# Where the operands of the large products begin in SBUF: a two-layer trunk with other offsets

## The chip, the core and the metric

The kernel runs on one core of a Trainium2 chip. Its metric is the device time of one execution in microseconds. Three runs of the kernel before gave 1264.4, 1265.62 and 1267.93 us, median 1265.62. One more execution, taken with the hardware profiler, is the one that every row below comes from.

The engines are named as the profile names them: PE is TensorE's matrix products, PEld is TensorE's loading of the stationary operand (it runs beside PE), DVE is VectorE, ACT is ScalarE, POOL is GpSimd, and SP is the engine that starts nearly all DMAs. SBUF is the on-chip memory of 128 partitions from which TensorE reads both operands; a tile's address below is its byte offset within each partition.

## The reference

Two residual layers on one sequence of 512 tokens with 1024 channels, in float32. Cut to what matters here, `h @ w` are the large products:

```python
mod = c_act @ ada_w[layer] + ada_b[layer]          # six shifts, scales and gates
h = rms_norm(x, norm_mix[layer]) * (1.0 + scale1) + shift1
if layer % 2 == 0:                                 # gated convolution and HGRN2 recurrence
    y = mixer_conv_hgrn(h, w_in_ab[j], conv_w[j], hg_norm[j], lower_bounds[layer], w_out_ab[j])
else:                                              # stick-breaking attention, 16 heads of 64
    y = mixer_stick_breaking(h, w_qkv[j], q_norm[j], k_norm[j], w_out_c[j])
x = x + gate1 * y
h = rms_norm(x, norm_mlp[layer]) * (1.0 + scale2) + shift2
x = x + gate2 * (jnp.square(jax.nn.relu(h @ mlp_w1[layer])) @ mlp_w2[layer])
```

## The kernel before

**Products.** Activations lie transposed, channels on the partitions and the 512 tokens along the row. Every large product is made of three: the weights and the activations are each split into a high part, rounded to TensorE's fast float32 form (`F32R`), and a low part, the rest. `mm3` (L281) issues, for one 128x128 block of weights, high weights by high activations (L284), high weights by low activations (L285) and low weights by high activations (L286). In each the weights are the stationary operand, loaded into the array, and the activations the moving operand, streamed through it. A product over all tokens is 512 columns wide; where a stage is cut into two halves of the tokens, so that the second half of the work before it can still be under way, it is 256 wide. In the attention's value products (`v_stream`, L1427 to L1429) and those of the first mixer (`v_g`, L737 to L739) the sides are exchanged: activations are stationary and weights move.

**Stages.** First norm and input products (`start`, L505); mixer of layer 0, whose chunked recurrence puts small products between the large ones (L701 to L947); its output projection, half of it in token halves (`proj`, L954); first MLP (`mlp_head` in halves, then `mlp` over 512 tokens, its last three outputs in halves); attention (L1088 to L1506); second MLP. From `start` on, the order of PE's instructions is the program's own or that of a list scheduler (`Graph`, L107), which orders by estimated durations and knows no addresses.

**Weights.** Each of the weight tiles, 128x1024 float32 (512 KB), is loaded by SP into one of three `raw` buffers, rounded by ACT into `whi` (L274) and subtracted by DVE into `wlo` (L275), each in a ring of four buffers.

**Where tiles lie.** A pool lays out its tiles one behind the other in the order of their first allocation, and the next pool begins where the last one ends: `base` (residual `x`, activations `hh`/`hl`, norms, constants), `wp` (`raw`, `whi`, `wlo`), `adap` (modulation), then `mix`, `mlp0`, `att` and `mlp1`, which take turns. So the size of every tile ahead sets where a tile begins. Four tiles matter only for that or are moved by the change: `gap0` (L319, 8 floats) and `gap1` (L320, 24 floats), which nothing reads or writes; `sel` (L248, 2048 bytes per partition), the stationary operand of eight products of layer 0's mixer (L899, L900); and `lvl` (L249, 448 bytes), masks that DVE reads in the same mixer (L805, L818).

Below, a tile's **place** is its address modulo 256 bytes. A block of 128 weight columns is 512 bytes, and a half of the tokens is 1024, so the blocks and halves of a tile have the place of the tile.

Of the kernel before, what the change touches and what calls it, by code (L numbers as in the profile page):

```python
# [12 lines left out]
F32 = mybir.dt.float32  # L13
F32R = mybir.dt.float32r
# [3 lines left out]
U8 = mybir.dt.uint8  # L18
# [4 lines left out]
P = 128  # L23
# [67 lines left out]
class Ring:  # L91
# [5 lines left out]
    def new(self):  # L97
        return Handle(self)
# [127 lines left out]
def trunk(tc, x_d, c_d, rep_d, small_d, const_d, ada_d, ws_d, win_d, wv_d, woab_d, w1_d, w2_d, wqk_d, wvc_d, woc_d, out_d):  # L226
# [6 lines left out]
    def pool(name, space=None, stack=es):  # L233
        kw = {} if space is None else {"space": space}
        return stack.enter_context(tc.tile_pool(name=name, bufs=1, reuse_waits="tile", **kw))

    base = pool("base")
    wp = pool("wp")
# [6 lines left out]
    modc = base.tile([P, 96], F32, name="modc")  # L245
    gsc = base.tile([P, 32], F32, name="gsc")
    lb = base.tile([P, 12], F32, name="lb")
    sel = base.tile([P, 512], F32R, name="sel")  # L248
    lvl = base.tile([P, 7 * 64], U8, name="lvl")  # L249
    ident = cons[:, C_ID:C_ID + P]  # L250
    ones = base.tile([P, P], F32, name="ones")
    o32 = cons[:, C_O32:C_O32 + 32]
# [16 lines left out]

    def split_w(raw, of=None):  # L270

        new = lambda n, tag: of[0].tile([P, 1024], F32R, name=n, tag=tag) if of else wp.tile([P, 1024], F32R, name=n, tag=n, bufs=4)
        hi, lo = [new(n, of and of[1 + i]) for i, n in enumerate(("whi", "wlo"))]
        act.copy(hi, raw)  # L274
        dve.tensor_tensor(lo, raw, hi.bitcast(F32), op=ALU.subtract)  # L275
        return hi, lo

    def load_w(src, of=None):
        return split_w(raw_w(src), of)
# [36 lines left out]
    eps_b = base.tile([P, 1], F32, name="eps_b")  # L316
    ls_b = base.tile([P, 1], F32, name="ls_b")

    base.tile([P, 8], F32, name="gap0")  # L319
    wp.tile([P, 24], F32, name="gap1")  # L320

    def rsqrt_act(ms, a, y):

# [16 lines left out]
    mp = pool("mix", stack=mx_s)  # L340
    mps_s = ExitStack()
    mps = pool("mps", PSUM, mps_s)

    def acc():
        return mps.tile([P, T], F32, name="acc", tag="acc", bufs=4)
# [55 lines left out]
    def late_constants():  # L401
        ctmp = wp.tile([P, 1024], F32, name="ctmp", tag="raw", bufs=3)
        act.dma_start(ctmp[:, :C_END - C_SEL], const_d[:, C_SEL:C_END])
        act.copy(sel, ctmp[:, 0:512])
        act.copy(sel4, cons[0:4, C_SEL4:C_SEL4 + P])
        act.copy(lvl, ctmp[:, 512:512 + 7 * 64])
# [256 lines left out]
        return hi, lo  # L663

    wv0 = start()
    start_s.close()
    late_constants()

# [424 lines left out]
    at_s, ap = ExitStack(), None  # L1093
# [72 lines left out]
    def spans_of(i):  # L1166


        spans, off = [], 0
        for i, b in enumerate(UNITS[i]):  # L1170
            spans.append((b, off, off + i, P * (b + 1)))
            off += P * (b + 1)
        return spans, off, off + len(spans)
# [3 lines left out]
    def open_attention():  # L1177

        nonlocal ap
        m_s.close()  # L1180
        adap_s.close()
        ap = pool("att", stack=at_s)

        pat, at = ap.tile([P, 2592], PAT, name="pat"), 0
        pool_e.memset(pat, 0.0)
        for i in range(3):
            spans, nn, nw = spans_of(i)
            pats.append(pat[:, at:at + 2 * nw])
            for j in range(2):
                for b, off, to, n in spans:  # L1190
                    pool_e.tensor_copy(pats[i][:, j * nw + to + P * b:j * nw + to + n], ident)
            at += 2 * nw
            for ts, name in ((om_t, "om"), (be_t, "be")):
                ts[i] = ap.tile([P, (2 * nw + 15) // 16 * 16], F32, name=f"{name}{i}")[:, :2 * nw]
                pool_e.memset(ts[i], 0.0)

    loads = []

# [265 lines left out]
    for hf in range(2):  # L1464
        for o in range(5, 8):
            order += [mm3h(tail[o, hf], whole, w_tail[o - 5], ks(k), (hid[k],), H[hf], False, k == 7, 256) for k in range(8)]
            on_dve(310, lambda o=o, hf=hf: x_add(o, tail[o, hf].t, H[hf], 0, GATE2), (tail[o, hf], xh[o, hf]), (xh[o, hf],), 0)
            nt_.add(o, hf)
        if hf:
            gate = G.op("HOST", 0.0, open_attention, after=[order[-1]])  # L1470
            for r in ap_rings:
                r.gate = gate
        finish([nt_.acc[hf]] + [nt_.sq[o, hf] for o in nin.direct], hf, 1, 0, ())
# [20 lines left out]
    for s_ in "v0 q2 q3 u0 u1 v1 w0 q4 v2 q5 u2 q6 u3 q7 v3 u4 u6 w1 u5 u7".split():  # L1494
        n = int(s_[1])
# [129 lines left out]
```

## Time and profile before

| what | us |
|---|---|
| median of three runs | 1265.62 |
| the profiled execution, whole time | 1265.67 |
| its span, from the first to the last instruction | 1263.9 |
| PE busy | 1243.3 (98%) |
| PEld busy | 1042.1 (82%) |
| DVE busy | 716.6 (57%) |
| ACT busy | 541.7 (43%) |

The busy times by stage, from the view that cuts the span into stretches:

| stretch, us | stage | PE busy | PEld busy | DVE busy | ACT busy |
|---|---|---|---|---|---|
| 0 to 40 | start | 31.50 | 25.86 | 32.64 | 16.70 |
| 40 to 245 | mixer of layer 0 | 202.65 | 166.30 | 158.18 | 70.97 |
| 288 to 590 | first MLP, 512 wide | 299.65 | 247.55 | 166.46 | 114.06 |
| 627 to 885 | attention | 255.76 | 202.58 | 176.67 | 168.66 |
| 885 to 931 | attention's output, norm, MLP head | 44.88 | 42.44 | 33.12 | 25.73 |

A PE instruction's busy time runs from its start to its modelled end, and the next one starts long before that end. So the mean duration of a product says little, and the distance from one start to the next is what a product costs in a row of products. The timeline's first column gives these starts to 0.01 us; over a row of equal products the distance is read from the first and the last start.

### The profile page before, as it was taken

The page shows a single profiled execution, that of the slowest core. Times are in us where ns is not written, and L with a number is a line of the kernel's source. Part 1 is how long each engine was busy: PE and PEld are TensorE (multiplying, and loading weights), DVE is VectorE, ACT ScalarE, POOL GpSimd, SP SyncE. Part 2 cuts the span into 40 slices and gives each one's busy share as a digit, 9 for nine tenths or more (in the row PEclk, how much of TensorE's full clock was granted, in tenths as well). Part 3 has the DMA queues.
Part 4 walks back from the last instruction along what each step waited for, and adds up shares of the span by engine and source line. Part 5 has one row for each costly group of instructions (what it writes and reads, how often), then busy time and mean ns, then how long its engine had stood idle before and what let it go on. Part 6 is the DMA issues. An engine that isn't in the chain of part 4 may idle for free.

```text
span 1263.9 us, 17038 instructions
## 1 busy us (share of the span) xinstructions
PE 1243.3 (98%) x6809; PEld 1042.1 (82%) x6809; DVE 716.6 (57%) x1107; ACT 541.7 (43%) x891; POOL 12.2 (1%) x24
## 2 busy tenths in 40 slices
PE   7999999999999999999999999999999999999998
PEld 6788877898878888888987778677988888888888
DVE  7897868576665656433667774669753322333321
ACT  4333233355441143622458755667465421355210
POOL 0000000000000000000200000000000000000000
PEclk9999999999999999999999999999999999999999
DMA  7665443415777666433232213223132233322330
GB/s 288 220 215 184 148 153 100 133 35 191 263 246 227 223 205 221 139 100 97 88 101 68 67 54 97 84 67 100 34 100 88 97 100 100 100 91 93 117 109 25
DMA packets 46607, 163.35 MB, mean 129 GB/s; under 512 B 5297, under 2 KB 6329, under 8 KB 46529
## 3 DMA queue, kind: packets, MB, share of 16 engines
q1 hardware_dynamic: 46384, 161.78, 39.6%
q8 instruction: 53, 0.87, 0.3%
q10 hardware_dynamic: 144, 0.49, 0.1%
q14 instruction: 26, 0.20, 0.1%
HBM read 155.96 MB, written 2.10 MB: 125 GB/s over the span
## 4 chain that ended last, share of the span: by engine, by line
PE 83%; DVE 6%; DMA 6%; ACT 3%; issue 1%; SPq 0%; DVEq 0%; ACTq 0%
PE b L284 20%; PE b L285 20%; PE b L286 20%; PE acc L284 3%; PE acc L286 3%; PE acc L285 3%; DMA wraw<-in_w 3%; PE b L1371 1%; PE b L1392 1%; DVE ascr L412 1%; PE b L1427 1%; DVE wlo L275 1%; PE b L1291 1%; ACT whi L274 1%; PE b L1428 1%; PE b L1429 1%
## 5 line engine op out<-in xcount | busy, mean ns | idle before, releaser
L274 ACT CAST whi<-wraw 128x1024 fp32r<-128x1024 f32 x150 | 157.7, 1054 | 448.2 <-PE b L285 255.9
L275 DVE TENSOR_TENSOR wlo<-wraw,whi 128x1024 fp32r<-128x1024 f32 x150 | 183.5, 1224 | 239.8 <-ACT whi L274 234.6
L284 PE MATMUL b<-hh,whi 128*128 128x512 f32 (+1 forms) x720 | 267.8, 372 | 1.8 <-ACT hh L1251 1.1
L286 PE MATMUL b<-hh,wlo 128*128 128x512 f32 (+1 forms) x720 | 263.0, 366 | 0.0
L285 PE MATMUL b<-hl,whi 128*128 128x512 f32 (+1 forms) x720 | 263.0, 366 | 0.0
L285 PE MATMUL b<-hidl,whi 128*128 128x512 f32 (+1 forms) x576 | 207.2, 360 | 1.9 <-DVE hidl L294 1.9
L284 PE MATMUL b<-hidh,whi 128*128 128x512 f32 (+1 forms) x576 | 207.4, 360 | 0.4 <-ACT hidh L293 0.4
L286 PE MATMUL b<-hidh,wlo 128*128 128x512 f32 (+1 forms) x576 | 207.1, 360 | 0.0
L284 PEld LDWEIGHTS b<-hh,whi 128*128 128x128 f32 x720 | 135.6, 188 | 30.2 <-issue 7.2
L286 PEld LDWEIGHTS b<-hh,wlo 128*128 128x128 f32 x720 | 135.5, 188 | 22.3
L285 PEld LDWEIGHTS b<-hl,whi 128*128 128x128 f32 x720 | 135.7, 189 | 21.5 <-DVE hl L1253 0.5
L412 DVE CUSTOM_DVE_ANT_0 ascr<-wraw,cb 128x1024 bf16<-128x1024 f32 x80 | 97.7, 1221 | 50.3 <-DMA wraw<-in_ada 50.2
L285 PEld LDWEIGHTS b<-hidl,whi 128*128 128x128 f32 x576 | 108.8, 189 | 18.6 <-DVE hidl L294 2.2
L284 PEld LDWEIGHTS b<-hidh,whi 128*128 128x128 f32 x576 | 108.8, 189 | 17.1 <-ACT hidh L293 0.9
L286 PEld LDWEIGHTS b<-hidh,wlo 128*128 128x128 f32 x576 | 108.8, 189 | 16.2
L498 DVE SCALAR_TENSOR_TENSOR x<-b,modc,x 128x512 f32<-128x512 f32 (+1 forms) x70 | 44.8, 641 | 96.9 <-PE b L286 96.8
L1205 DVE TENSOR_TENSOR wlo<-raw,whi 128x1024 fp32r<-128x1024 f32 x33 | 40.3, 1222 | 30.5 <-ACT whi L1204 30.3
L294 DVE TENSOR_TENSOR hidl<-relu,hidh 128x512 fp32r<-128x512 f32 (+1 forms) x64 | 42.4, 665 | 22.8 <-ACT hidh L293 22.8
L284 PE MATMUL acc<-hh,whi 128*128 128x512 f32 x128 | 52.3, 408 | 0.0
L286 PE MATMUL acc<-hh,wlo 128*128 128x512 f32 x128 | 50.0, 391 | 0.0
L285 PE MATMUL acc<-hl,whi 128*128 128x512 f32 x128 | 49.9, 390 | 0.0
L1355 DVE TENSOR_TENSOR_SCAN om<-om,pat 128x772 f32<-128x772 f32 (+2 forms) x24 | 46.5, 1936 | 5.8 <-ACT om L1351 5.8
(335 smaller groups left out, 1786.7 us busy)
## 6 DMA issues: line engine op xcount, KB each, us to landing
wraw<-in_w SPq DMA_DIRECT2D x125, 512.0 KB, 3.5
wraw<-in_ada SPq DMA_DIRECT2D x80, 512.0 KB, 4.3
eraw<-in_ada SPq DMA_DIRECT2D x16, 512.0 KB, 5.6
wraw<-in_win SPq DMA_DIRECT2D x16, 512.0 KB, 3.6
raw<-in_wqk SPq DMA_DIRECT2D x16, 512.0 KB, 3.6
raw<-in_ws SPq DMA_DIRECT2D x8, 512.0 KB, 6.3
wraw<-in_woab SPq DMA_DIRECT2D x8, 512.0 KB, 3.4
raw<-in_wvc SPq DMA_DIRECT2D x8, 512.0 KB, 3.4
```

The lines of the kernel that those rows point to most:

```text
L274: act.copy(hi, raw)
L275: dve.tensor_tensor(lo, raw, hi.bitcast(F32), op=ALU.subtract)
L284: pe.matmul(ps, whi, h[0][:, hs], start=start, stop=False)
L285: pe.matmul(ps, whi, h[1][:, hs], start=False, stop=False)
L286: pe.matmul(ps, wlo, h[0][:, hs], start=False, stop=stop)
L294: dve.tensor_tensor(lo[:, sl], t_[:, sl], hi[:, sl].bitcast(F32), op=ALU.subtract)
L412: dve.tensor_tensor_reduce(out=scr, in0=raw, in1=cb, scale=1.0, scalar=0.0, op0=ALU.mult, op1=ALU.add, accum_out=modr[:, col:col + 1])
L498: dve.scalar_tensor_tensor(x[o][:, sl], ps, mcol(l, v, o), x[o][:, sl], op0=ALU.mult, op1=ALU.add)
L1205: on_dve(1024, lambda: dve.tensor_tensor(lo.t, raw.t, hi.t.bitcast(F32), op=ALU.subtract), (raw, hi), (lo,), 1)
L1291: on_pe(0.13, lambda s=s, sq=sqs[p, s, s0]: pe.matmul(ms.t[64 + 32 * s:96 + 32 * s, sl], hs, sq.t[:, sl], start=True, stop=True), (sqs[p, ...
L1355: on_dve(2 * nw, lambda: dve.tensor_tensor_scan(s_(), s_(), pats[i][:, ::-1], 0.0, op0=ALU.mult, op1=ALU.max), (om,), (om,), 2)
L1371: pe.transpose(tp.t[:, o_:o_ + P], be.t[:, w0:w0 + P], ident)
```

## The change

No operation is added, removed or put in another place: the rows of PE, PEld, DVE, ACT, POOL and SP stand in the same order with the same shapes before and after. What differs is where tiles lie in SBUF.

```diff
-    sel = base.tile([P, 512], F32R, name="sel")
-    lvl = base.tile([P, 7 * 64], U8, name="lvl")
...
-        new = lambda n, tag: of[0].tile([P, 1024], F32R, name=n, tag=tag) if of else wp.tile([P, 1024], F32R, name=n, tag=n, bufs=4)
+        new = lambda n, tag: (of[0].tile([P, 1088], F32R, name=n, tag=tag)[:, 16:1040] if of else
+                              wp.tile([P, 1024], F32R, name=n, tag=n, bufs=4))
...
-    base.tile([P, 8], F32, name="gap0")
-    wp.tile([P, 24], F32, name="gap1")
+    base.tile([P, 56], F32, name="gap0")
+    wp.tile([P, 40], F32, name="gap1")
...
     mps = pool("mps", PSUM, mps_s)
+    sel = mp.tile([P, 512], F32R, name="sel")
+    lvl = mp.tile([P, 7 * 64], U8, name="lvl")
+    mp.tile([P, 16], F32, name="gap2")
...
     wv0 = start()
+    wp.tile([P, 48], F32, name="gap3")
     start_s.close()
...
                 pool_e.memset(ts[i], 0.0)
+        ap.tile([P, 32], F32, name="gap4")
```

The second hunk concerns four weight tiles of the output projection (outputs 5 and 6) that lie in free mixer tiles instead of the ring. The places that come out, in bytes past a multiple of 256:

| operands | lines | before: moving, stationary | after: moving, stationary |
|---|---|---|---|
| `hh`/`hl`, `hidh`/`hidl`, `yy`, `ybh`/`ybl` by `whi`/`wlo` | L284 to L286, L645, L651 | 32, 32 | 32, 96 |
| `oT` by `whi`/`wlo` | L284 to L286 | 160, 32 | 32, 96 |
| `oT` by weights in `stq` | L284 to L286 | 160, 224 | 32, 96 |
| `stk` by `stq` | L1343, L1344 | 160, 224 | 32, 96 |
| `whi`/`wlo` by `hh`/`hl` | L737 to L739, L1427 to L1429 | 32, 32 | 96, 32 |
| `hidh`/`hidl` by weights kept in `hidh`/`hidl` (`Joined`, L206) | L284 to L286 | 32, 32 | 32, 32 |
| `ehl` by `sel` | L899, L900 | 32, 192 | 32, 32 |

## The prediction

> **What bounds the kernel now.** I read the page first: busy times, then the chain of work that ended last.
>
> ```profile
> span 1263.9 us, 17038 instructions
> PE 1243.3 (98%) x6809; PEld 1042.1 (82%) x6809; DVE 716.6 (57%) x1107; ACT 541.7 (43%) x891; POOL 12.2 (1%) x24
> PE 83%; DVE 6%; DMA 6%; ACT 3%; issue 1%; SPq 0%; DVEq 0%; ACTq 0%
> ```
>
> PE carries 83% of the chain. Next the view of who waited for whom, of PE alone; its largest rows outside the start are these:
>
> ```profile
> PE b L285 <- DVE hidl L294: 1.9, 1, 1.9
> PE b L1371 <- DVE be L1357: 1.8, 3, 0.9
> PE b L284 <- ACT hh L1251: 1.1, 1, 1.1
> ```
>
> No wait of PE in the two MLPs or the attention is above 2 us. So PE's own pace sets the time after the start, and what the change can do is alter the distance between PE's starts. It adds no instruction, so it can do nothing else on the path. Then the same matter by stage:
>
> ```profile
> core 0: us, PE busy (x) PEld busy (x) DVE busy (x) ACT busy (x) POOL busy (x), PEclk, DMA share, GB/s
> 245.00:288.00 43.00, 42.32 (x345) 41.87 (x344) 27.27 (x60) 19.09 (x43) 0.00 (x0) 1.00 0.12 38
> 590.00:627.00 37.00, 37.00 (x308) 36.90 (x307) 18.17 (x32) 14.27 (x23) 6.04 (x11) 1.00 0.31 100
> 931.00:1226.00 295.00, 295.00 (x1304) 244.27 (x1303) 96.79 (x97) 109.33 (x146) 0.00 (x0) 1.00 0.32 104
> 1226.00:1264.00 38.00, 34.52 (x288) 34.32 (x287) 7.33 (x10) 2.93 (x3) 0.00 (x0) 1.00 0.08 28
> ```
>
> In the stretches with 256-wide products (245, 590, 1226) the weight loading is busy as long as PE; in a 512-wide one (931) it has room. The granted clock is 1.00 in all of them.
>
> **The pace now.** From the timeline, the first and last start of three rows of back-to-back products: 512 wide and 256 wide with both operands at place 32, then 256 wide with the moving operand at 160 and the stationary one at 224.
>
> ```profile
> 499.80 0.39 PE L286 MATMUL b<-hh,wlo 128*128 128x512 f32 x1
> ...
> 501.84 0.39 PE L286 MATMUL b<-hh,wlo 128*128 128x512 f32 x1
> 590.02 0.28 PE L286 MATMUL b<-hidh,wlo 128*128 128x256 f32 x1
> ...
> 591.94 0.28 PE L284 MATMUL b<-hidh,whi 128*128 128x256 f32 x1
> 890.67 0.28 PE L284 MATMUL b<-oT,stq 128*128 128x256 f32 x1
> ...
> 892.71 0.28 PE L284 MATMUL b<-oT,stq 128*128 128x256 f32 x1
> ```
>
> These are 9, 16 and 18 steps: 2.04/9 = 226.7 ns, 1.92/16 = 120.0 ns, 2.04/18 = 113.3 ns. The last two are the same operation and shape, and differ in where operands begin: a stationary place 0 or 64 bytes past the moving one. The change gives nearly all large products a difference of 64. The view of groups, weight loads alone, shows the same two stretches (590 to 615 and 891 to 896):
>
> ```profile
> L286 PEld LDWEIGHTS b<-hidh,wlo 128*128 128x128 f32 x56 | 10.7, 192 | 0.0
> L284 PEld LDWEIGHTS b<-oT,stq 128*128 128x128 f32 x13 | 2.4, 188 | 0.0
> ```
>
> A load takes 192 ns at difference 0 and 188 at 64. My reading: the load of the next block's weights starts with the stream of the present one, and where both begin at the same place they meet in the memory and the load is held up. A 256-wide product hides no such delay; a 512-wide one has 107 ns more.
>
> [...]
>
> **The change part by part.** First the 256-wide products that go from difference 0 to 64.
>
> ```profile
> L284 PE MATMUL b<-hh,whi 128*128 128x256 f32 x160 | 47.2, 295 | 1.8 <-ACT hh L1251 1.1 <-DVE x L498 0.7
> L284 PE MATMUL b<-hidh,whi 128*128 128x256 f32 x160 | 45.5, 284 | 0.0
> L284 PE MATMUL acc<-yy,whi 128*128 128x256 f32 x32 | 9.2, 289 | 0.0
> L1427 PE MATMUL b<-whi,hh 128*128 128x256 f32 x128 | 38.1, 298 | 0.0
> ```
>
> The first three rows have two siblings each (L285, L286), and `ybh`/`ybl` have as many as `yy`: 3 x 160 + 3 x 160 + 6 x 32 = 1152 products. At 120.0 - 113.3 = 6.7 ns each that is 7.7 us. I take off 1.0: in the attention's first half the products do not all stand at 120 now, and part of what is won ahead of a wait of the kind shown above is waited away. Term: **-6.7 us**; bounds 0 and -7.7.
>
> The value products (fourth row, 3 x 128) become moving 96, stationary 32, a difference of 192. No row shows that for a long run; the nearest two are the 120.0 they have and 113.3. I keep 120: **0**, bounds 0 and -2.6 (384 x 6.7 ns).
>
> Then the 512-wide ones, which are far more:
>
> ```profile
> L284 PE MATMUL b<-hh,whi 128*128 128x512 f32 x560 | 220.9, 395 | 0.0
> L284 PE MATMUL b<-hidh,whi 128*128 128x512 f32 x416 | 161.9, 389 | 0.4 <-ACT hidh L293 0.4
> L284 PE MATMUL acc<-hh,whi 128*128 128x512 f32 x128 | 52.3, 408 | 0.0
> ```
>
> With their siblings 3 x (560 + 416 + 128) = 3312. What they do at difference 64 is the open question, one nanosecond each being 3.3 us. Rows at 64 exist only in the attention:
>
> ```profile
> 739.21 0.39 PE L1343 MATMUL b<-stk,stq 128*128 128x512 f32 x1
> 739.44 0.39 PE L1344 MATMUL b<-stk,stq 128*128 128x512 f32 x1
> 739.67 0.39 PE L284 MATMUL b<-oT,whi 128*128 128x512 f32 x1
> ...
> 848.32 0.33 PE L1343 MATMUL b<-stk,stq 128*128 128x384 f32 x1
> 848.49 0.34 PE L1344 MATMUL b<-stk,stq 128*128 128x384 f32 x1
> ```
>
> The 512-wide pair steps 0.23 us, that is 230 rather than 226.7 ns. The 384-wide step after a row of 256-wide ones is 0.17 us. Per column: 113.3/256 = 0.443 ns, 170/384 = 0.443, and the settled 226.7/512 = 0.443. So at 64 the cost is proportional to the columns where it has settled, and 512 columns would be 226.7, as now. As for the 230: it is a pair between other products, and 512-wide products at difference 0 behave alike after an interruption:
>
> ```profile
> 756.48 0.40 PE L285 MATMUL b<-hl,whi 128*128 128x512 f32 x1
> ...
> 758.56 0.39 PE L285 MATMUL b<-hl,whi 128*128 128x512 f32 x1
> 758.79 0.39 PE L286 MATMUL b<-hh,wlo 128*128 128x512 f32 x1
> 759.02 0.39 PE L284 MATMUL b<-hh,whi 128*128 128x512 f32 x1
> 759.24 0.39 PE L285 MATMUL b<-hl,whi 128*128 128x512 f32 x1
> 759.47 0.39 PE L286 MATMUL b<-hh,wlo 128*128 128x512 f32 x1
> ```
>
> Nine steps take 2.08 us, 231 ns each; only then do they settle (758.79 to 759.47: 227). So a pair at 230 tells little of a long row. Term: **0**; bounds from -6.7 ns (as the 256-wide ones) to +3.3 ns each, -22 to +11 us.
>
> The attention's output products have a difference of 128 now and do not settle:
>
> ```profile
> 732.61 0.39 PE L284 MATMUL b<-oT,whi 128*128 128x512 f32 x1
> ...
> 733.78 0.40 PE L286 MATMUL b<-oT,wlo 128*128 128x512 f32 x1
> ```
>
> Five steps in 1.17 us, 234 ns. There are 120 of them and 48 256-wide ones; short rows between other work, so I count some 2.5 ns each: **-0.3 us**, bounds 0 and -1. The 256-wide products of the start wait for ACT and DVE: 0. `sel`, `lvl` and the gap tiles add no instruction and no wait of PE: 0.
>
> Sum: -6.7 - 0.3 = -7.0 us. From the profiled execution's 1265.67 (span 1263.9 and 1.8 around it; the median of the runs, 1265.62, is the same) that gives **1258.7 us**. The 6.7 us come in four places where nothing hides them or fills in: 245 to 288, 590 to 627, around the attention's ends, and 1226 to the end. DVE and ACT, at 57% and 43%, must supply weights sooner there, but a 256-wide stage uses each weight tile twice and asks them for half as much per product.
>
> **The rivals.** *Slower: the 512-wide products do not settle at difference 64.* They would go on at 230, or at the 231 to 234 of the unsettled rows above. For: every 512-wide row seen at 64 or 128 is at 230 or more, and none at 226.7. Against: none is longer than a pair at 64, and the columns' proportion. Price: 3312 x 3.3 = 10.9 us at 230, 17.5 at 232; time 1258.7 + 10.9 = 1269.6, to 1276. It decides from 7.0/3312 = 2.1 ns per product on. If only the rows that are interrupted (mixer, attention, by my estimate some 1,000 of the products) stay at 230, it is 1258.7 + 3.3 = 1262.
>
> *Faster still: the 512-wide ones also lose 6.7 ns.* 3312 x 6.7 = 22.2 us, 1236.5. Against: 0.443 ns per column is the best pace in any row of these rounded products. [...]
>
> *No change: the difference of places is not the cause.* The 113.3 stretch also differs in having place 160, in its time and its neighbours. Then nothing moves: 1265.7.
>
> **How the numbers follow.** Forecast (256-wide won, 512-wide as now), 1255 to 1261.5: 0.50. Faster still, below 1255: 0.08. No change, or part of the 512-wide rows unsettled, 1262 to 1269: 0.22. Slower, above 1269.4: 0.20, half of it above 1273. A measurement of this kernel tells 0.3% from no change, 3.8 us: faster (below 1261.8) 0.58, same 0.22, slower 0.20. The range leaves out the faster case and the upper half of the slower one: 1254 to 1273.
>
> **What the profile after would show.** In the halved stretches (590 and 1226) steps of 113.3 ns and loads of 188 ns if the first term is right, 120 and 192 if not. In the second MLP (931 to 1226 now) steps of 226.7 if the forecast is right, 230 or more if the slower rival is, 220 if the faster one is. In the value products 120 or less. The prediction is wrong above all if a long 512-wide row settles at another step than 226.7: that term has 3312 products behind it and only pairs of rows to go by.

## The result: slower by 0.9%, where faster by 0.6% was forecast

| | median, us | range of the runs, us | against before |
|---|---|---|---|
| before | 1265.01 | 1262.07 to 1267.93 | |
| after | 1276.88 | 1275.23 to 1277.97 | ratio 1.0093, interval 1.0076 to 1.0109 |

The change costs 11.9 us. The forecast was 1258.7 us and its range ended at 1273, so the time lies outside it, on the side of the slower rival.

The page of the kernel after, its first lines and the engines' shares of the chain of waits (the profiled execution took 1277.97 us):

```profile
span 1276.2 us, 17038 instructions
PE 1257.8 (99%) x6809; PEld 1034.6 (81%) x6809; DVE 717.1 (56%) x1107; ACT 541.1 (42%) x891; POOL 12.2 (1%) x24
PE 85%; DMA 6%; DVE 5%; ACT 3%; issue 1%; SPq 0%; DVEq 0%; ACTq 0%
```

There are as many instructions as before on every engine. PE is busy 14.5 us longer (1243.3 before), and the loading of weights 7.5 us shorter (1042.1). The waits of PE behind the start, from the view of who waited for whom, are those of before, the second one shorter than its 1.9 us:

```profile
PE b L1375 <- DVE be L1361: 1.8, 3, 0.8
PE b L284 <- DVE hidl L293: 1.5, 1, 1.5
PE b L283 <- ACT hh L1255: 1.1, 1, 1.1
```

So no new wait explains the loss. What did change is the distance between PE's starts. The timeline after, at the places that answer to those of the prediction (`mm3` has moved up one line, to L283 to L285): 512-wide products with the moving operand at 32 and the stationary one at 96, 256-wide ones with the same places, and the output projection, also 256 wide with the same places.

```profile
504.18 0.39 PE L284 MATMUL b<-hl,whi 128*128 128x512 f32 x1
...
506.98 0.39 PE L284 MATMUL b<-hl,whi 128*128 128x512 f32 x1
598.32 0.28 PE L285 MATMUL b<-hidh,wlo 128*128 128x256 f32 x1
...
600.36 0.28 PE L285 MATMUL b<-hidh,wlo 128*128 128x256 f32 x1
249.84 0.28 PE L284 MATMUL acc<-ybl,whi 128*128 128x256 f32 x1
...
252.19 0.28 PE L283 MATMUL acc<-ybh,whi 128*128 128x256 f32 x1
```

These are 12, 18 and 20 steps: 2.80/12 = 233.3 ns for 512 columns (226.7 before), 2.04/18 = 113.3 for 256 (120.0 before), and 2.35/20 = 117.5 in the projection. The weight loads of the second row, from the view of groups between 597.5 and 617 us, are at the 188 ns that were forecast:

```profile
L285 PEld LDWEIGHTS b<-hidh,wlo 128*128 128x128 f32 x56 | 10.5, 188 | 0.0
```

The long 512-wide stretch of the second MLP shows the same in the view that cuts the span into stretches; in 295 us there are 1266 products where the stretch of before (931 to 1226) had 1304, and the clock is 1.00 in both:

```profile
945.00:1240.00 295.00, 295.00 (x1266) 236.41 (x1265) 92.52 (x93) 102.72 (x136) 0.00 (x0) 1.00 0.30 98
```

To see where all the time went, the distances from each PE start to the next are added up by kind over the whole timeline. A distance over 1.2 times the pace is cut at the pace (227 or 120 ns), and its rest counts as waiting.

| PE's time, us | products | before | after | difference |
|---|---|---|---|---|
| 512 wide, activations moving | 3736 | 849.3 | 870.8 | +21.5 |
| 256 wide, activations moving | 1519 | 181.1 | 175.0 | -6.1 |
| weights moving, 512 wide and 256 wide | 480 | 67.6 | 67.3 | -0.3 |
| waiting in front of these | | 31.6 | 30.5 | -1.1 |
| all other work | | 129.3 | 127.7 | -1.6 |
| sum, to the last start | | 1259.0 | 1271.3 | +12.3 |

The first row is the loss, the second the forecast gain. Of the first, +19.9 us lies in the 3312 products of the prediction's 512-wide term (752.3 us before, 772.2 after); of the second, -5.8 lies in the 1152 of its 256-wide term.

### The profile page after: what moved, and what is told of

Read it like the earlier page. It is cut to its first block, busy times and chain, and to the rows that moved or that the text cites. A ratio compares the mean times of both kernels' runs of the same rounds, so it can differ in the third digit from the quotient of the medians.

```text
span 1276.2 us, 17038 instructions
## 1 busy us (share of the span) xinstructions
PE 1257.8 (99%) x6809; PEld 1034.6 (81%) x6809; DVE 717.1 (56%) x1107; ACT 541.1 (42%) x891; POOL 12.2 (1%) x24
## 4 chain that ended last, share of the span: by engine, by line
PE 85%; DMA 6%; DVE 5%; ACT 3%; issue 1%; SPq 0%; DVEq 0%; ACTq 0%
PE b L283 20%; PE b L284 20%; PE b L285 20%; PE acc L283 3%; PE acc L285 3%; PE acc L284 3%; DMA wraw<-in_w 3%; PE b L1375 1%; PE b L1396 1%; DVE wlo L274 1%; PE b L1431 1%; PE b L1295 1%; DVE ascr L414 1%; ACT whi L273 1%; PE b L1433 1%; PE b L1432 1%
## 5 line engine op out<-in xcount | busy, mean ns | idle before, releaser
L283 PE MATMUL b<-hh,whi 128*128 128x512 f32 (+1 forms) x720 | 269.6, 375 | 2.0 <-ACT hh L1255 1.1
L284 PE MATMUL b<-hl,whi 128*128 128x512 f32 (+1 forms) x720 | 265.0, 369 | 0.0
L285 PE MATMUL b<-hh,wlo 128*128 128x512 f32 (+1 forms) x720 | 264.8, 368 | 0.0
L284 PE MATMUL b<-hidl,whi 128*128 128x512 f32 (+1 forms) x576 | 208.2, 361 | 1.5 <-DVE hidl L293 1.5
L283 PE MATMUL b<-hidh,whi 128*128 128x512 f32 (+1 forms) x576 | 208.3, 362 | 0.0
L285 PE MATMUL b<-hidh,wlo 128*128 128x512 f32 (+1 forms) x576 | 208.1, 361 | 0.0
L283 PEld LDWEIGHTS b<-hh,whi 128*128 128x128 f32 x720 | 134.9, 187 | 34.1 <-issue 7.2
L285 PEld LDWEIGHTS b<-hh,wlo 128*128 128x128 f32 x720 | 134.9, 188 | 25.7
L284 PEld LDWEIGHTS b<-hl,whi 128*128 128x128 f32 x720 | 134.9, 188 | 24.8 <-DVE hl L1257 0.5
L284 PEld LDWEIGHTS b<-hidl,whi 128*128 128x128 f32 x576 | 107.8, 187 | 21.2 <-DVE hidl L293 1.9
L283 PEld LDWEIGHTS b<-hidh,whi 128*128 128x128 f32 x576 | 107.8, 187 | 19.4
L414 DVE CUSTOM_DVE_ANT_0 ascr<-wraw,cb 128x1024 bf16<-128x1024 f32 x80 | 97.7, 1222 | 45.7 <-DMA wraw<-in_ada 45.2
L285 PEld LDWEIGHTS b<-hidh,wlo 128*128 128x128 f32 x576 | 107.8, 187 | 19.2
L283 PE MATMUL acc<-hh,whi 128*128 128x512 f32 x128 | 52.9, 413 | 0.0
L284 PE MATMUL acc<-hl,whi 128*128 128x512 f32 x128 | 50.6, 395 | 0.0
L285 PE MATMUL acc<-hh,wlo 128*128 128x512 f32 x128 | 50.6, 395 | 0.0
```

Source lines behind the costliest of these rows:

```text
L283: pe.matmul(ps, whi, h[0][:, hs], start=start, stop=False)
L284: pe.matmul(ps, whi, h[1][:, hs], start=False, stop=False)
L285: pe.matmul(ps, wlo, h[0][:, hs], start=False, stop=stop)
L414: dve.tensor_tensor_reduce(out=scr, in0=raw, in1=cb, scale=1.0, scalar=0.0, op0=ALU.mult, op1=ALU.add, accum_out=modr[:, col:col + 1])
```

## The experiments

Three theories were put against each other. *Theory 1*: the difference between the stationary and the moving place sets the pace, as the prediction assumed, but with its own sign for each width. *Theory 2*: the stationary operand's place 96 costs by itself, wherever the moving one is. *Theory 3*: something else in the change, such as the constants moved into the mixer's pool.

**A map of places.** A kernel of its own runs rows of 48 equal products, each row with another pair of places:

```diff
+PAIRS = ([(32, (32 + 16 * j) % 256) for j in range(16)] +
+         [(m, (m + d) % 256) for m in (0, 16, 64, 96, 160, 224) for d in (0, 64)])
...
+                    pe.matmul(o, W[0][:, w], M[0][:, v], start=first, stop=False)
+                    pe.matmul(o, W[0][:, w], M[1][:, v], start=False, stop=False)
+                    pe.matmul(o, W[1][:, w], M[0][:, v], start=False, stop=last)
```

> This kernel leaves out the whole trunk and computes only products of slices of the input: for each of 28 pairs of places (moving, stationary, in bytes past a multiple of 256) 48 products 512 wide and then 48 products 256 wide, back to back, three to a block of weights as in the kernel. Sixteen pairs keep the moving operand at 32 and put the stationary one at 32, 48, 64 and so on in steps of 16; twelve put the moving one at 0, 16, 64, 96, 160 and 224 with a difference of 0 and of 64. Theory 1, the difference of the two places sets the pace: at difference 0 every 512-wide row steps 226.7 ns and every 256-wide row 120.0, at difference 64 every 512-wide row 233.3 and every 256-wide row 113.3, whatever the moving place is. Theory 2, the place of the stationary operand itself counts: the rows with the stationary operand at 96 step 233.3 and 113.3, those at 32 step 226.7 and 120.0, and the rows with the moving operand at 0, 16, 64, 160 and 224 do not repeat the figures of 32 at the same difference. Theory 3, something else in the kernel (the traffic of the other engines, DMAs, the moved constants) makes the pace: all 512-wide rows here step alike, and all 256-wide rows too.

From its timeline, the first and last start of the last 30 steps of five rows, in this order: 512 wide at (moving, stationary) (32, 32), 256 wide at (32, 32), 512 wide at (32, 96), 256 wide at (32, 96), and 256 wide at (16, 80).

```profile
12.50 0.39 PE L48 MATMUL b<-m,w 128*128 128x512 f32 x1
...
19.30 0.39 PE L48 MATMUL b<-m,w 128*128 128x512 f32 x1
21.56 0.28 PE L48 MATMUL b<-m,w 128*128 128x256 f32 x1
...
25.16 0.28 PE L48 MATMUL b<-m,w 128*128 128x256 f32 x1
79.89 0.39 PE L48 MATMUL b<-m,w 128*128 128x512 f32 x1
...
86.89 0.39 PE L48 MATMUL b<-m,w 128*128 128x512 f32 x1
89.12 0.28 PE L48 MATMUL b<-m,w 128*128 128x256 f32 x1
...
92.65 0.28 PE L48 MATMUL b<-m,w 128*128 128x256 f32 x1
340.59 0.28 PE L48 MATMUL b<-m,w 128*128 128x256 f32 x1
...
343.99 0.28 PE L48 MATMUL b<-m,w 128*128 128x256 f32 x1
```

Divided by 30 these are 226.7, 120.0, 233.3, 117.7 and 113.3 ns. DVE does nothing beside these rows, and ACT nothing before 421 us, where results begin to be copied out; between the shown rows DMA moves 1 GB/s at most. So the places alone can make the paces of the kernels before and after. All rows, read in the same way:

| moving place | difference 0: 512, 256 wide | difference 64: 512, 256 wide |
|---|---|---|
| 32 | 226.7, 120.0 | 233.3, 117.8 |
| 0, 64, 96, 160, 224 (each the same) | 226.7, 120.0 | 233.3, 113.3 |
| 16 | 233.3, 118.3 | 226.7, 113.3 |

With the moving operand at a multiple of 32, the difference (0 or 64) decides at 512 columns, as theory 1 has it, and theories 2 and 3 fall: the stationary place 96 gives 226.7 with the moving operand at 96 and 233.3 with it at 32. Theory 1 missed twice: at 256 columns (32, 96) stepped 117.8 where 113.3 was expected, and at 16 the difference alone does not decide. The other fourteen stationary places beside a moving 32 gave 226.7 for 512 columns at two of them only (16 and 176), 229.8 to 234.2 at the rest, and 116.7 to 120.0 for 256. No row of the map was below 226.7 or 113.3.

**The change with its difference taken back, in two ways.** One kernel keeps the stationary place 96 and brings the activations there too; the other keeps all of the change but puts the weight ring back at 32. Both against the kernel after:

```diff
 both at 96:
-    base.tile([P, 56], F32, name="gap0")
-    wp.tile([P, 40], F32, name="gap1")
+    base.tile([P, 72], F32, name="gap0")
+    wp.tile([P, 24], F32, name="gap1")
 ring at 32:
-    wp.tile([P, 40], F32, name="gap1")
+    wp.tile([P, 24], F32, name="gap1")
 in both:
-        new = lambda n, tag: (of[0].tile([P, 1088], F32R, name=n, tag=tag)[:, 16:1040] if of else
+        new = lambda n, tag: (of[0].tile([P, 1088], F32R, name=n, tag=tag)[:, :1024] if of else
...
-    wp.tile([P, 48], F32, name="gap3")
```

> The kernel after with everything 64 bytes further on and the weight ring as far as the activations: moving and stationary operands of the large products both begin at 96, difference 0. Theory 1 (the difference sets the pace): 512-wide rows back at 226.7 ns, 256-wide rows back at 120.0, time 1264 to 1267 us, ratio to the kernel before 0.999 to 1.001. Theory 2 (the stationary operand's own place 96 is what costs): 233.3 and 113.3 stay, 1275 to 1278 us, ratio 1.008 to 1.011. Theory 3 (the moved constants or another tile): as after, 1275 to 1278.

> The kernel after with only the weight ring put back 64 bytes, to place 32; the moved constants and all gaps that place the other tiles stay as after. Large products have a difference of 0 again, products of the attention's own operands (stk by stq) keep 64. Theory 1 and theory 2 alike: 512-wide rows 226.7 ns, 256-wide rows 120.0, 1264 to 1267 us, ratio 0.999 to 1.001. Theory 3 (the moved constants or another tile cost the time): stays at 1275 to 1278 us, ratio 1.008 to 1.011.

Measured: both at 96 took 1264.82 us, ratio to before 1.0005 (0.9995 to 1.0015); the ring at 32 took 1265.67 us, ratio 1.0007 (0.9995 to 1.0019). The timeline of the kernel with both at 96, in the two stages of the rows above:

```profile
499.61 0.39 PE L284 MATMUL b<-hl,whi 128*128 128x512 f32 x1
...
501.88 0.39 PE L285 MATMUL b<-hh,wlo 128*128 128x512 f32 x1
594.78 0.28 PE L284 MATMUL b<-hidl,whi 128*128 128x256 f32 x1
...
597.18 0.28 PE L283 MATMUL b<-hidh,whi 128*128 128x256 f32 x1
```

2.27/10 = 227 ns and 2.40/20 = 120.0. The whole loss goes with the difference, and so does the gain. The moved constants, the longer gaps and the shift of all other tiles cost nothing that can be measured; the wider of the two intervals reaches 0.19%, 2.4 us.

**How far the rule reaches.** A second map: more places, the widths between 256 and 512, and repeats.

```diff
+ROWS = ([(16, (16 + 16 * j) % 256, n) for j in range(1, 16) if j != 4 for n in (512, 256)] +
+        [(m, (m + 64) % 256, n) for m in (48, 80, 112, 144, 176, 208, 240) for n in (512, 256)] +
+        [(m, s, n) for n in (288, 320, 352, 384, 416, 448, 480) for m, s in ((32, 32), (32, 96), (16, 80))] +
+        [(m, s, n) for r in range(3) for m, s, n in ((32, 96, 256), (16, 80, 512), (16, 80, 256), (32, 96, 512))])
```

> This kernel leaves out the whole trunk and, like the map before it, only runs rows of 48 equal products of slices of the input. First the moving operand at 16 with the stationary one at the other multiples of 16; then the moving one at 48, 80, 112, 144, 176, 208 and 240 with a difference of 64, 512 and 256 wide; then widths of 288 to 480 in steps of 32 at (moving, stationary) (32, 32), (32, 96) and (16, 80); then three repeats of (32, 96) and (16, 80) at both widths in turn. Of the first map (32, 32) had 226.7 and 120.0 ns, (32, 96) 233.3 and 117.8, (16, 80) 226.7 and 113.3. Theory 1b, the difference and the moving place modulo 32 set the pace: every moving place here that is an odd multiple of 16 steps 226.7 and 113.3 at difference 64, as (16, 80) did. Theory 1c, a pace is a state that a row falls into, decided by how it begins: the repeats of one pair differ from each other, and the places 48 to 240 show 226.7 at some and 233.3 at others. On the widths: if the time is proportional to the columns, as the prediction took it, all widths at (32, 96) step 0.443 ns per column, 127.5 at 288, 170 at 384, 212.5 at 480; if an amount is added per product, 6.7 ns over (32, 32) at every width; if the pace goes in steps of 6.67 ns, only multiples of 6.67 occur in rows that settle, and the sign of the difference between the two pairs changes with the width.

Its timeline, the last 30 steps at 384 columns, (32, 32) and then (32, 96), and of a repeat of 256 columns at (32, 96):

```profile
425.21 0.33 PE L47 MATMUL b<-m,w 128*128 128x384 f32 x1
...
430.41 0.34 PE L47 MATMUL b<-m,w 128*128 128x384 f32 x1
433.59 0.34 PE L47 MATMUL b<-m,w 128*128 128x384 f32 x1
...
438.89 0.34 PE L47 MATMUL b<-m,w 128*128 128x384 f32 x1
603.39 0.28 PE L47 MATMUL b<-m,w 128*128 128x256 f32 x1
...
606.79 0.28 PE L47 MATMUL b<-m,w 128*128 128x256 f32 x1
```

| columns | (32, 32), ns | (32, 96), ns | ns per column at (32, 96) |
|---|---|---|---|
| 256 | 120.0 | 113.3 | 0.443 |
| 288 | 131.8 | 133.3 | 0.463 |
| 320 | 146.7 | 146.7 | 0.458 |
| 352 | 161.1 | 160.0 | 0.455 |
| 384 | 173.3 | 176.7 | 0.460 |
| 416 | 188.2 | 186.7 | 0.449 |
| 448 | 206.7 | 202.2 | 0.451 |
| 480 | 216.7 | 216.0 | 0.450 |
| 512 | 226.7 | 233.3 | 0.456 |

The (32, 32) values at 256 and 512 columns are those of the first map. The proportion by which the prediction went does not exist: 0.443 ns per column holds at (32, 96) for 256 columns only, and which pair is the faster changes from width to width. Nor is it an amount added per product. Nor do only multiples of 6.67 ns occur (131.8, 161.1 and 176.7 are none), though the sign does change with the width, as the third expectation had it.

On the repeats, theories 1b and 1c both missed. Against 1b, the moving places 48 to 240 in steps of 32 stepped 113.3, but 228.9 rather than 226.7. Against 1c, repeats within this map agree: (32, 96) at 256 columns stepped 113.3 and (16, 80) at 512 columns 228.9, three times each. Yet the first map had 117.8 and 226.7 for these two pairs, so the places do not fix the pace of every pair. Each map was executed once, on a chip of its own; what sets the two maps apart stays open. The rows of (32, 32) and (32, 96) at 512 columns, on the other hand, settled at the same pace whenever they ran, 226.7 (once, in a later map, 227.2) and 233.3 ns.

**A place for each width.** If the two widths want different differences, the weights can be placed by use. The tiles of the ring become 256 bytes longer, the ring stands at 32, and a weight tile is a slice that begins at 32 for 512-wide products, at 96 for 256-wide ones, and at 224 where weights move in the attention's value products. The core of the edit, against the kernel after; a second kernel turns the choice round.

```diff
-    def split_w(raw, of=None):
+    def split_w(raw, of=None, at=0):
...
-                              wp.tile([P, 1024], F32R, name=n, tag=n, bufs=4))
+                              wp.tile([P, 1088], F32R, name=n, tag=n, bufs=4)[:, at:at + 1024])
...
-    ws = {o: load_w(woab_d[o], PLACES.get(o)) for o in HALVED}
+    ws = {o: load_w(woab_d[o], PLACES.get(o), 16) for o in HALVED}
...
-            w = load_w(w2_d[l, 1, o, 0])
+            w = load_w(w2_d[l, 1, o, 0], at=16)
...
-        w, ops, h = [weights(wvc_d[g, c]) for c in range(2)], [], hh
+        w, ops, h = [weights(wvc_d[g, c], at=48) for c in range(2)], [], hh
```

> The kernel after with the weight ring back at place 32, its tiles 256 bytes longer, and a slice chosen by use: weights of 512-wide products at 32 (difference 0), those of 256-wide products at 96 (difference 64), the moving weights of the attention's value products at 224 (difference 64). The theory that the two widths want different differences, by the steps measured in rows: 512-wide 226.7, 256-wide 113.3 to 117.8; 1152 to 1536 products gain 2.2 to 6.7 ns, 2.5 to 10 us less than before: 1254 to 1262 us, ratio 0.992 to 0.998. If the 6.7 ns of the 256-wide products are waited away in the kernel, or longer tiles cost something: 1264 to 1267, ratio 0.999 to 1.002.

> The same kernel with the choice turned round: weights of 512-wide products at 96 (difference 64), those of 256-wide products and of the value products at 32 (difference 0). If the two widths' costs simply add up, this kernel and the mixed one lie as far above and below: after minus before was 11.9 us, so swap minus before is that plus what the mixed one gains, 14 to 22 us: 1279 to 1287 us, ratio 1.011 to 1.018. If the loss of the kernel after came from anything but the 512-wide products' difference: near before, ratio under 1.005.

Measured: the mixed kernel 1261.85 us, ratio 0.9970 (0.9953 to 0.9987); the one turned round 1280.88, ratio 1.0130 (1.0106 to 1.0154). Both lie in the ranges of the first theory, and their differences from before (-3.3 and +15.7 us, medians against the 1265.18 of their own series) add up to 12.4, close to the 11.9 of the change, which has both. The mixed kernel gave less than its steps: by the same sum of starts as above, its 256-wide products won 3.6 us and its value products 1.5, but waiting in front of 512-wide products grew by 3.5. The view of PE's waits between 340 and 400 us, and two stretches there:

```profile
PE b L285 <- ACT hidh L294: 1.5, 1, 1.5
PE b L286 <- DVE hidl L295: 1.3, 1, 1.3
370.00:380.00 10.00, 10.00 (x32) 8.03 (x33) 5.21 (x8) 2.10 (x2) 0.00 (x0) 0.71 0.69 252
380.00:390.00 10.00, 10.00 (x45) 8.26 (x44) 5.68 (x8) 2.10 (x2) 0.00 (x0) 1.00 0.68 220
```

PE waits for the last hidden tile of the first MLP's first half, and from 370 to 380 us the mean clock is 0.71, with 32 products where the next 10 us hold 45. The timeline of PE shows both waits (in brackets) and the slow steps behind them:

```profile
367.98 0.50 PE L285 MATMUL b<-hidh,whi 128*128 128x512 f32 x1 [1.54 <-ACT hidh L294]
369.80 0.80 PE L286 MATMUL b<-hidl,whi 128*128 128x512 f32 x1 [1.32 <-DVE hidl L295]
370.39 0.63 PE L287 MATMUL b<-hidh,wlo 128*128 128x512 f32 x1
...
375.51 0.55 PE L287 MATMUL b<-hidh,wlo 128*128 128x512 f32 x1
```

The timeline of DVE says why the tile is late:

```profile
366.78 1.23 DVE L276 TENSOR_TENSOR wlo<-wraw,whi 128x1024 fp32r<-128x1024 f32 x1 [0.38 <-ACT whi L275]
367.92 1.22 DVE L416 CUSTOM_DVE_ANT_0 ascr<-wraw,cb 128x1024 bf16<-128x1024 f32 x1
369.06 0.08 DVE L416 DVE_READ_ACCUMULATOR2_ANT modr<- 128x1 f32 x1
369.06 0.68 DVE L295 TENSOR_TENSOR hidl<-relu,hidh 128x512 fp32r<-128x512 f32 x1
```

`hidl` stands on DVE behind a weight split and a dot product of the modulation (L416).

**Which operand the next one meets.** The prediction's reading was that the load of the next weights collides with the present stream. This map separates a product's own pair of places from the pair that its stream makes with the next product's weights:

```diff
+CYCLES = {"A": [(32, 32)], "B": [(32, 96)], "C": [(0, 0), (64, 64), (128, 128), (192, 192)],
+          "D": [(192, 0), (128, 192), (64, 128), (0, 64)], "E": [(32, 32), (32, 96)]}
```

> This kernel leaves out the whole trunk and runs rows of 48 products of slices of the input, 512 and 256 wide, in five patterns, each four times in another order: A (moving 32, stationary 32), B (32, 96), C the pairs (0, 0), (64, 64), (128, 128), (192, 192) in turn, D the pairs (192, 0), (128, 192), (64, 128), (0, 64) in turn, E the pairs (32, 32), (32, 96) in turn. In C every product has difference 0 to its own weights, but the next product's weights lie 64 past the operand that streams; in D every product has difference 64 to its own weights, and the next product's weights lie at the place of the operand that streams. A and B as in the maps before: 226.7 and 120.0, 233.3 and 113.3 to 117.8. If what counts is the load of the next weights beside the present stream (the prediction's reading): C steps like B (233.3, 113.3 to 118), D like A (226.7, 120.0). If the product's own pair counts: C like A, D like B. If the places of successive products count in another way still: neither.

Measured, the mean of the last 36 steps, each pattern four times:

| pattern | own, next | 512 wide, ns | 256 wide, ns |
|---|---|---|---|
| A | 0, 0 | 226.7 (once 227.2) | 120.0 |
| B | 64, 64 | 233.3 | 113.3 |
| C | 0, 64 | 228.3 (once 230.6) | 118.1 to 118.6 |
| D | 64, 0 | 233.0 to 233.1 | 117.3 to 117.5 |
| E | 0 and 64 in turn | 230.0 to 232.6 | 116.7 to 118.3 |

Neither reading is borne out in full. At 512 columns C is nearer to A and D to B, as a product's own pair would have it, against the prediction's reading; at 256 columns both lie between. In C and D both places also change from product to product, which they do not in A and B; no pattern separates that. Whether load and stream meet in the memory at all stays open.

**The wait that hid a part.** Last, six of the modulation pieces are taken from in front of that hidden tile and done in the second half of the MLP, in the mixed kernel, in the kernel before, and in the kernel after:

```diff
-                if j > 5:
+                if j > 3 if hb else 5 < j < 13:
                     background(2)
```

> The mixed kernel with six of the modulation pieces (one DMA of 512 KB and one DVE dot product each) taken out of the first MLP's tiles 13 to 15 and done in its second half, so that DVE's copy of the last hidden tile no longer stands behind dot products that wait for their DMA. If the wait of PE at 365 us (3.7 us and a slower clock after it in the mixed kernel's profile, 2.9 us in before's) is what hid a part of the gain: it goes, 1256 to 1260 us, ratio 0.993 to 0.996. If the wait only moves elsewhere: as mixed, 1261 to 1263, ratio 0.996 to 0.999.

> The kernel before with the same six modulation pieces moved, and nothing else. If the wait at 365 us ends the path there: 2 to 3 us less than before, 1262 to 1263.5, ratio 0.997 to 0.9985; if it moves elsewhere: 1264 to 1266, ratio 0.999 to 1.001. The difference between this kernel and the mixed one with the same move is then the operands' places alone: by the steps 5 to 9 us.

> The kernel after with the same six modulation pieces moved, and nothing else. From the starts of PE's products in the profiles, the places alone cost 21.5 us in 512-wide products and give 6.7 us in 256-wide ones, 15 us together, of which after shows 12 because PE, being slower, waits less at 365 us (1.5 us instead of 2.3, and no slow clock). If that is so, the move gives after less than it gave before (1264.56 to 1260.28, 4.3 us): 1 to 3 us, time 1273.5 to 1276, ratio 1.007 to 1.009, and the distance to the kernel before with the same move grows to 13.5 to 16 us. If the waits have nothing to do with the pace: 4 us as before, 1272 to 1273, ratio 1.006, and the distance stays 12.

Each ratio is to the kernel before as it ran in the same series (medians 1263.86 to 1265.18 us).

| places | as it was, us, ratio to before | pieces moved, us, ratio to before |
|---|---|---|
| before | 1264.56, 1 | 1260.28, 0.9965 (0.9952 to 0.9977) |
| after | 1276.88, 1.0093 (1.0076 to 1.0109) | 1276.45, 1.0099 (1.0082 to 1.0115) |
| mixed | 1261.85, 0.9970 (0.9953 to 0.9987) | 1254.53, 0.9918 (0.9905 to 0.9931) |

The waits between 340 and 400 us are gone in all three profiles with the pieces moved. In the mixed kernel PE is now busy through the whole stretch from 360 to 380 us:

```profile
360.00:380.00 20.00, 20.00 (x90) 16.58 (x89) 10.75 (x14) 4.21 (x4) 0.00 (x0) 1.00 0.70 233
```

The same stretch of the kernel before, with its waits of 1.9 and 0.4 us:

```profile
360.00:380.00 20.00, 17.65 (x77) 14.06 (x76) 12.10 (x19) 6.02 (x8) 0.00 (x0) 1.00 0.79 256
```

All three times lie outside the ranges given for the case that the wait goes: the mixed kernel 1.5 us below its 1256 to 1260, the one before 1.7 us below its 1262 to 1263.5, the one after 0.5 us above its 1273.5 to 1276. By the medians the move gives 7.3 us in the mixed kernel, 4.3 in the one before and 0.4 in the one after, where 1 to 3 was expected; each interval reaches about 2 us to either side.

What is the move's own can be read from the profiled executions, one for each kernel: the start of PE's 1801st product, ahead of the moved pieces, and that of its 2101st, behind the wait.

| places | as it was: from, to, us between | pieces moved: from, to, us between | difference, us |
|---|---|---|---|
| before | 338.20, 409.13, 70.93 | 335.32, 403.32, 68.00 | -2.9 |
| after | 340.05, 411.77, 71.72 | 340.82, 410.82, 70.00 | -1.7 |
| mixed | 335.90, 410.18, 74.28 | 333.87, 401.87, 68.00 | -6.3 |

With the pieces moved, the 300 steps take 300 x 226.7 ns, or 300 x 233.3 in the kernel after, and no more. Behind this stretch each two executions agree within 0.5 us. Whatever else sets them apart arises ahead of it, where the move changes nothing: 2.9 and 2.0 us less in before and mixed, 0.8 more in after.

So, in these single executions, the wait and what came behind it cost most in the mixed kernel (6.3 us), whose PE came there first and then ran slowly (twelve steps of 427 ns), and least in the kernel after (1.7 us), whose slower PE (steps of 233.3 ns) hid a part of the wait. By the stretch, it hid 2.9 - 1.7 = 1.2 us of what the change costs, 13.1 rather than 11.9. The medians with the pieces moved give 1276.45 - 1260.28 = 16.2 us (13.5 to 16 was expected), from two series; that the 3 us beyond 13.1 have to do with the wait is not shown. Places by width give 1260.28 - 1254.53 = 5.8 us, within one series. The mixed kernel with the pieces moved beats both kernels of this case, by 0.8% the one before.

## Why the prediction was wrong, by its own steps

**What bounds the kernel: right in the main.** PE's pace moved the time (+21.5, -6.1 and -0.3 us in the table of starts), and no new wait arose behind the start. But that no wait is above 2 us said too little of the one at 365 us: without it, its stretch of the kernel before is 2.9 us shorter, and by the table above it hid 1.2 us of the loss.

**The 256-wide term: right.** Forecast -6.7 us, measured -5.8 in its 1152 products. The MLPs' tails (their last three outputs), the first MLP's head and most of the attention's first products went to 113.3 ns as forecast; the output projection's 192 products and the second MLP's head (48 products from 930.56 to 936.21 us) only to 117.5 to 117.8, which was not foreseen. That the sum still fits is partly luck: the 1.0 us taken off for waits and for the attention covers these 240 products, which lack some 4.5 ns each (1.1 us).

**The value products: right within the bounds.** Forecast 0, bounds 0 and -2.6. Both rows in which weights move make -0.3 together: 256 wide 45.8 us before and 45.2 after, 512 wide 21.8 and 22.1. The attention's output products, forecast at -0.3 us, stayed within 0.1 us of what they were.

**The 512-wide term: wrong, and this step decided it.** Forecast 0, measured +19.9 us in its 3312 products (+21.5 in all 512-wide ones), beyond its bound of +11. It rested on two readings. "So at 64 the cost is proportional to the columns where it has settled, and 512 columns would be 226.7": the second map shows no such proportion, 0.460 ns per column at 384 and 0.456 at 512. The row it was read from was one step of 0.17 us on a column rounded to 0.01 and behind 256-wide products; settled rows of 384 columns at (32, 96) step 0.177. And "a pair at 230 tells little of a long row": the pair was the better witness; the settled pace lies 3 ns above it, not below. That a row at difference 0 starts at 231 and then settles at 226.7 shows only that those places settle there.

**The slower rival: the right products and the right direction, priced too low.** "The 512-wide products do not settle at difference 64" at 230 or 232 was given 1269.6 to 1276 us and a chance of 0.20. They settle, but at 233.3; 3312 x 6.7 = 22.1 us would have given 1281, and less waiting and other work (-2.7 in the table of starts) brought it to the profiled 1278. What should have carried weight was its own evidence: every 512-wide row seen at 64 or 128 stood at 230 or more.

**"The difference of places is not the cause": refuted**, by both operands at 96 and by the ring at 32.

**The reading behind it is not shown.** That load and stream meet in the memory explains neither why 512 columns are slower with the weights apart nor patterns C and D. Nor do the loads of a 512-wide stretch follow the pace. Here they are before (497 to 552 us, difference 0, steps of 226.7 ns) and after (505 to 560 us, difference 64, steps of 233.3):

```profile
L284 PEld LDWEIGHTS b<-hh,whi 128*128 128x128 f32 x56 | 10.5, 188 | 2.1
L283 PEld LDWEIGHTS b<-hh,whi 128*128 128x128 f32 x52 | 9.7, 187 | 2.4
```

A load is 1 ns shorter where the product steps 6.7 ns longer, so a longer load is not what made these products slow. What does is open: the same products at 226.7 or 233.3 ns by places alone show that where operands begin matters, and not by which mechanism.

## What to carry to other kernels

Where operands of back-to-back products begin was worth 3% of a 512-wide step here (226.7 ns at places (32, 32), 233.3 at (32, 96)) and 6% of a 256-wide one (120.0 and 113.3), in opposite directions, so a pair of places read from one width must not be carried to another: run the rows that the kernel has, at each width, by themselves, and place operands by use. Read a settled pace over tens of steps, never from a pair. And where an engine that sets the pace becomes faster, look for the wait that its slowness had been hiding: in the mixed kernel PE waited 2.86 us for the last hidden tile, in the one before 2.35.

## What the runs showed of the hardware

- **Steady rows of one pair stepped in units of about 6.67 ns.** Every row of the first two maps whose last 30 steps differ by no more than 1 ns is a multiple of it: 113.3 is 17, 120.0 is 18, 146.7 is 22, 160.0 is 24, 173.3 is 26, 186.7 is 28, 206.7 is 31, 226.7 is 34 and 233.3 is 35 units. The other rows vary from step to step; 228.9 at (16, 80), for one, repeats 225, 231, 231. Where places change from product to product, steady steps need not be multiples: C stood at 228.3, and E at 256 columns once at 116.7. What makes the unit was not tried.
- **One pair of places had two paces.** (32, 96) at 256 columns stood at 117.5 to 117.8 in the first map, in the output projection and in the tails of the mixed kernel, and at 113.3 in the other maps and the tails of the kernel after. In the kernel after it changed within the attention's first products, all at the same places: 14 steps from 631.92 to 633.57 us are 117.9 ns each, and, after a few small products of the norm (L1242) between them, 66 steps from 635.97 to 643.45 us are 113.3. What decides it was not found. It is not the row in front: one of the same places, 512 wide, stood ahead of the 117.8 of the first map and ahead of two of the three 113.3 in the second and all four in the third.
- **A slow stretch stood behind two short waits, in one execution.** In the mixed kernel's timeline, PE started a product at 367.98 us after 1.54 us without work and the next at 369.80 after 1.32 more, and then twelve 512-wide products stepped 427 ns (370.39 to 375.51, 5.1 us) instead of 227, 2.4 us more; the mean clock from 370 to 380 us was 0.71. In before, waits of 0.45 and 1.90 us at the same place were followed by a clock of 1.00. With the pieces moved, the mixed kernel had no such wait and a clock of 1.00 from 360 to 380 us. That the waits are what lowered the clock is not shown.
